# A two-layer hybrid encoder trunk: calls recorded, list-scheduled in the kernel and emitted as one fixed list

## The chip, the core and the metric

One core of one Trainium2 chip runs the whole kernel in one launch. Times are device microseconds of that core. A core has five engines with a queue each: PE (TensorE, matmuls), DVE (VectorE), ACT (ScalarE), POOL (GpSimd) and SP (SyncE, which here only issues DMAs). Each engine takes its instructions in order; between engines they are ordered by semaphores that one instruction raises when it has ended and another waits for.

## The reference, cut to what matters

Two layers (DEPTH = 2) over 512 tokens of width 1024, float32. Each layer is:

```python
h = rms_norm(x, norm_mix[l])
proj = h @ w_in[l]                          # 1024 -> 3224 columns
y_att = attention_mixer(...)                # windowed softmax attention, 6 heads
y_dn  = deltanet_mixer(...)                 # gated DeltaNet, chunked, two directions
y_rw  = rwkv_mixer(...)                     # RWKV-7 time mixing, two directions
x = x + concatenate([y_att, y_dn, y_rw]) @ w_out[l]     # 1024 -> 1024
h = rms_norm(x, norm_ffn[l])
u = depthwise_conv(h @ ffn_w_up[l], conv_w)             # 1024 -> 5632
gate, val = split(u)
x = x + (silu(gate) * val) @ ffn_w_down[l]              # 2816 -> 1024
```

A last `rms_norm` closes the trunk.

## The kernel before, in words

Activations lie transposed: 128 channels on the partitions, 512 tokens along the free axis. Every large product is made column block by column block: for 128 output channels, `weights` loads 512 rows of the weight at a time (256 KB, tile `wr`) by a DMA on SP's queue, ACT rounds it to a high part `wh` (L321), POOL makes the low part `wl` (L322), and `product` issues three matmuls of 128x128 by 128x512 for each 128 rows: `wh` with the high part of the activation (`hh`), `wh` with its low part (`hl`), `wl` with `hh` (L332 to L334). `wr`, `wh` and `wl` have three buffers each. Per layer there are 26 column blocks of the input projection with 8 such triples each, 8 of the output projection with 8, 44 of the up-projection with 8 and 8 of the down-projection with 22: 800 triples, and 4,800 matmuls in both layers.

The stages of a layer follow each other: the input projection for RWKV (`proj`, `token_shift`), `rwkv_prep` twice, `dn_gates`, `dn_proj`, a 32x32 triangular inverse on DVE (`invert`, `finish_inverse`), the eight serial steps of `rwkv_scan`, `dn_prep`, the inverse for DeltaNet (`invert_both`), the eight steps of `dn_scan` with the attention heads beside it, `dn_out`, the output projection, the gated MLP (L1074 to L1097) and the down-projection (L1101 to L1105). The mixers consist of some 3,500 small float32 matmul calls in both layers and of elementwise work on DVE, ACT and POOL.

The order of the work: the code calls the engines directly (`V`, `S`, `G`, `PE`, `nc.sync`), and the framework's `TileContext(nc, auto_bufs=True)` (L1148) orders the calls itself when it closes, engine by engine, by its own cost model; it puts in a wait wherever an instruction reads or overwrites what another one made. Work of different engines and DMAs runs side by side as far as these waits let it.

Of the kernel before, what the change touches and what calls it, by code (L numbers as in the profile page):

```python
# [14 lines left out]
P = 128  # L15
# [99 lines left out]

def trunk(tc, t, out):
    nc = tc.nc
    V, S, G, PE = nc.vector, nc.scalar, nc.gpsimd, nc.tensor
# [16 lines left out]
    def ps(stream, shape=(P, T)):  # L135
        return psp.tile(list(shape), F32, tag="ps" + stream, bufs=PS_BUFS[stream], name=nm("ps"))

    def p4(*free, dt=F32):
        return bp.tile([P, *free], dt, tag="p4", bufs=20, name=nm("p4"))

    def t2(stream, *free, dt=F32):
        return bp.tile([P, *(free or (T,))], dt, tag="t" + stream, bufs=T_BUFS[stream], name=nm("t" + stream))

    def cv(*free, dt=F32):
        return bp.tile([P, *(free or (T,))], dt, tag="cv", bufs=8, name=nm("cv"))

    def at_(*free, dt=F32):
        return bp.tile([P, *(free or (T,))], dt, tag="at", bufs=5, name=nm("at"))
# [3 lines left out]
    def sm(*free):  # L152
        n = math.prod(free)
        a = bp.tile([P, T], F32, tag="sm", bufs=7, name=nm("sm"))[:, :n]
        return a.rearrange("p (a b) -> p a b", b=free[1])
# [3 lines left out]
    def tiny(*free, tag="tiny"):  # L159
        if len(free) > 1:  # L160
            lo = W + DEPTH * NPAR + 2 * T + 48 * small_at.setdefault(tag, len(small_at))
            names = " ".join("abc"[: len(free)])
            return fixed[:, lo : lo + math.prod(free)].rearrange(f"p ({names}) -> p {names}", **dict(zip("abc", free)))
        return bp.tile([P, *free], F32, tag=tag, bufs=1 if len(free) > 1 else 3, name=nm(tag))
# [7 lines left out]
    nc.sync.dma_start(par[:, :, :n1], t["params"][:, :, :n1])  # L172
# [30 lines left out]

    def late_params():
        nc.sync.dma_start(cst[:, n0:], t["consts"][:, n0:])
        nc.sync.dma_start(par_all[:, :, n1:], t["params"][:, :, n1:])
        for l in range(DEPTH):
            nc.sync.dma_start(sinkb[l], t["attn_sink"][l].unsqueeze(0).broadcast_to([P, 6]))
# [19 lines left out]
    def exp_ln_tables():  # L228
        tc.keep_in_program_order(S.preload_act_table_set("natural_log_exp_and_others"))
# [7 lines left out]

    def rotary_tables():
        pi_ = t2("d", T, dt=I32)
        nc.sync.dma_start(pi_, t["positions"].broadcast_to([P, T]))  # L240
# [21 lines left out]
    def split(src, gcol, tag, k):  # L262
        hi = bp.tile([P, T], F32R, tag=f"hh{k}", bufs=1, name=nm("hh"))
        lo = bp.tile([P, T], F32R, tag=f"hl{k}", bufs=1, name=nm("hl"))
        if gcol is None:
            S.activation(hi, src, AF.Copy)
            V.tensor_tensor(lo, src, hi.bitcast(F32), sub)
        else:
            S.activation(hi, src, AF.Copy, scale=gcol)
            V.scalar_tensor_tensor(lo, src, gcol, hi.bitcast(F32), mult, sub)  # L270
        return hi, lo

    class Norm:
# [32 lines left out]
    def weights(pieces, nk, m=P):  # L306


        parts = []
        for k0 in range(0, nk, WK):  # L310
            k1 = min(nk, k0 + WK)
            n = k1 - k0
            if ahead:
                raw = ahead.pop(0)
            else:
                raw = bp.tile([P, WK, m], F32, tag="wr", bufs=3, name=nm("wr"))
                for dst, src in pieces(raw[:, :n, :], k0, k1):
                    nc.sync.dma_start(dst, src)
            hi = bp.tile([P, WK, m], F32R, tag="wh", bufs=3, name=nm("wh"))
            lo = bp.tile([P, WK, m], F32R, tag="wl", bufs=3, name=nm("wl"))  # L320
            S.activation(hi[:, :n, :], raw[:, :n, :], AF.Copy)  # L321
            G.tensor_tensor(lo[:, :n, :], raw[:, :n, :], hi[:, :n, :].bitcast(F32), sub)  # L322
            parts += [(hi[:, k, :], lo[:, k, :]) for k in range(n)]
        return parts

    def product(o, w, x):


        n = len(w)
        for k in range(n):  # L330
            (wh, wl), (xh, xl) = w[k], x[k]
            PE.matmul(o, wh, xh, start=k == 0, stop=False)  # L332
            PE.matmul(o, wh, xl, start=False, stop=False)  # L333
            PE.matmul(o, wl, xh, start=False, stop=k == n - 1)  # L334

    def proj(l, parts, c0, m=P, heads=None):
# [53 lines left out]

    def invert(dpk, upper, E, work):
# [29 lines left out]

    def invert_both(dpks, work):
# [21 lines left out]

    def finish_inverse(st, o1, o2, units, upper, sign):
# [25 lines left out]

    def token_shift(l, o, i, rb, dst):
# [6 lines left out]

    def rwkv_prep(l, pr_, st, wau):  # L480
# [35 lines left out]
        nc.sync.dma_start(st["aside"][:, pr_, :], bv)  # L516
# [84 lines left out]

    def rwkv_scan(st):
# [56 lines left out]

    def rwkv_out(l, st, pr_, dst):  # L660
        y = st["y"][:, pr_, :]
        bv, g = t2("r"), t2("r")
        nc.sync.dma_start(bv, st["aside"][:, pr_, :])
        nc.sync.dma_start(g, st["aside"][:, 2 + pr_, :])
# [32 lines left out]

    def dn_gates(l, o, rb, scr, st):
# [19 lines left out]
        nc.scalar.dma_start(scr[0:6], rt[0:6])  # L718
        nc.scalar.dma_start(scr[6:12], rt[38:44])
# [9 lines left out]

    def dn_prep(l, pr_, st, qkv, nb, scr):  # L730
# [13 lines left out]
        for hh in range(2):  # L744
            nc.scalar.dma_start(e[64 * hh : 64 * hh + 64], sv[2 * pr_ + hh].unsqueeze(0).broadcast_to([64, 2, T]))
# [31 lines left out]

    def dn_scan(st):
# [71 lines left out]

    def dn_out(l, st, pr_, zs):
# [21 lines left out]

    def attn_head(l, tq, q, k, vt, dst):
# [37 lines left out]
    def layer(l, norm, xd, last):  # L912
# [9 lines left out]
        for i in range(8):  # L922
# [6 lines left out]
            if i == 3:  # L929
                wau = bp.tile([P, 2, 256], F32, tag="wau", name=nm("wau"))  # L930
                nc.sync.dma_start(wau[0:64], t["rw_w_up"][l].rearrange("d r c -> r d c"))
                nc.sync.dma_start(wau[64:128], t["rw_a_up"][l].rearrange("d r c -> r d c"))
                gup = bp.tile([P, T], F32, tag="gup", name=nm("gup"))[:, :256]
                nc.sync.dma_start(gup, t["rw_g_up"][l])
# [7 lines left out]
        for pr_ in range(2):  # L942
# [4 lines left out]
            nc.sync.dma_start(rw["aside"][:, 2 + pr_, :], g)  # L947
# [3 lines left out]

        def attn_proj():
# [18 lines left out]

        def gate_proj(pr_, z):
# [11 lines left out]

        def dn_proj(pr_):
# [69 lines left out]
        for j in range(KT):  # L1055
# [9 lines left out]
            nc.sync.dma_start(xo, xd[:, j, :])  # L1065
# [47 lines left out]
    for l in range(DEPTH):  # L1113
        x, norm = layer(l, norm, xd, l == DEPTH - 1)
        xd = xdram
        if l < DEPTH - 1:
            for k in range(KT):
                nc.sync.dma_start(xd[:, k, :], x[k])
    nfw = at["norm_final"]
    for k in range(KT):  # L1120
        V.scalar_tensor_tensor(x[k], x[k], par[0][:, nfw + k : nfw + k + 1], norm.rb, mult, mult)
        nc.sync.dma_start(out[:, k, :], x[k])
# [29 lines left out]
```

## Time and profile before

| | |
|---|---|
| median of three runs | 1716.09 us (1713.92 to 1722.8) |
| the profiled execution | 1722.8 us, span 1721.0 us |
| granted TensorE clock, mean over the span | 0.931 of full speed |
| PE busy | 1544.2 us |
| DVE / ACT / POOL busy | 973.5 / 792.0 / 638.7 us |
| mixers of layer 0, then of layer 1 | 0 to 464 us, 866 to 1306 us |
| up-projection with the gated MLP, layer 0 | 508 to 746 us |

The span is from the first to the last instruction; what lies around it is 1.8 us. Busy times of the engines overlap each other, so their sum is far above the span. A matmul's record overlaps the next one's, since matmuls are pipelined: the distance between starts tells the rate. In views by stretch, PEclk is the mean granted clock as a share of full speed; 1.00 is 2.4 GHz and 0.50 is 1.2 GHz. A line such as L322 is the line of the kernel that issued the instruction.

### The profile page before, as it was taken

What the parts mean: (1) busy time and instruction counts of PE and PEld (TensorE: products, weight loads), DVE (VectorE), ACT (ScalarE), POOL (GpSimd) and SP (SyncE); (2) the same over time, 40 slices, a digit from 0 to 9 for tenths busy, and PEclk for the clock granted to TensorE, in tenths of its full rate; (3) what the DMA queues carried; (4) which work ended last, traced back from release to release, by engine and by line L of the source; (5) the groups of instructions that cost most, each with busy time, mean ns of one, the idle gap of its engine ahead of it and who ended that gap; (6) DMA issues with size and microseconds to landing.
All of it is one profiled execution on the core that took longest, in us unless ns stands there. A gap on an engine that the chain in (4) does not pass through costs nothing. (4 is left out here: it accounts for less than half of the span.)

```text
span 1721.0 us, 29049 instructions
## 1 busy us (share of the span) xinstructions
PE 1544.2 (90%) x11500; PEld 1208.7 (70%) x11500; DVE 973.5 (57%) x1595; ACT 792.0 (46%) x1493; POOL 638.7 (37%) x510
## 2 busy tenths in 40 slices
PE   7988889569999999999998887983899999999997
PEld 4676666347778888888876666652677788888885
DVE  6578946875535557731136797579563555555001
ACT  5547453355444444433336654351734544444321
POOL 4321323101265554445552112420104555555553
PEclk9989979669999999999999998995799999999998
DMA  6221211100143333333442012220003333333331
GB/s 185 73 57 38 56 38 44 37 2 20 36 122 96 98 98 95 96 104 114 119 101 68 25 45 50 55 70 1 4 19 93 102 95 97 98 99 114 101 101 65
DMA packets 230536, 126.07 MB, mean 73 GB/s; under 512 B 23656, under 2 KB 221416, under 8 KB 230400
## 3 DMA queue, kind: packets, MB, share of 16 engines
q1 hardware_dynamic: 228624, 121.02, 25.0%
q10 hardware_dynamic: 1776, 3.20, 0.6%
q8 instruction: 90, 1.47, 0.3%
q14 instruction: 46, 0.38, 0.1%
HBM read 117.84 MB, written 6.34 MB: 72 GB/s over the span
## 5 line engine op out<-in xcount | busy, mean ns | idle before, releaser
L322 POOL TENSOR_TENSOR wl<-wr,wh 128x512 fp32r<-128x512 f32 (+1 forms) x408 | 553.6, 1363 | 753.2 <-ACT wh L321 664.2
L332 PE MATMUL ps<-hh,wh 128*128 128x512 f32 x1248 | 505.2, 405 | 22.1 <-ACT wh L321 19.6
L333 PE MATMUL ps<-hl,wh 128*128 128x512 f32 x1248 | 504.5, 404 | 0.0
L334 PE MATMUL ps<-hh,wl 128*128 128x512 f32 x1248 | 500.9, 401 | 0.4 <-POOL wl L322 0.4
L321 ACT ACTIVATE wh<-wr 128x512 fp32r<-128x512 f32 (+1 forms) x408 | 246.2, 615 | 330.8 <-PE ps L333 262.4
L332 PEld LDWEIGHTS ps<-hh,wh 128*128 128x128 f32 x1248 | 237.8, 191 | 80.9 <-ACT wh L321 20.4
L333 PEld LDWEIGHTS ps<-hl,wh 128*128 128x128 f32 x1248 | 238.0, 191 | 56.8 <-issue 4.2
L334 PEld LDWEIGHTS ps<-hh,wl 128*128 128x128 f32 x1248 | 237.5, 190 | 56.8 <-issue 3.9
L1104 DVE TENSOR_TENSOR p<-ps,p 128x512 f32<-128x512 f32 x16 | 11.1, 692 | 196.6 <-PE ps L334 196.6
L332 PE MATMUL ps<-p,wh 128*128 128x512 f32 x256 | 99.6, 389 | 0.0
L333 PE MATMUL ps<-p,wh 128*128 128x512 f32 x256 | 99.6, 389 | 0.0
L334 PE MATMUL ps<-p,wl 128*128 128x512 f32 x256 | 99.6, 389 | 0.0
L903 PE MATMUL ps<-fixed,cv 128*128 128x128 f32 x120 | 24.9, 340 | 62.4 <-DVE cv L900 62.0
L1081 DVE TENSOR_TENSOR tr<-ps,rb 128x512 f32<-128x512 f32 x44 | 30.4, 691 | 80.9 <-PE ps L334 80.8
L292 POOL TENSOR_TENSOR tr<-tr,tr 128x512 f32<-128x512 f32 x32 | 42.6, 1332 | 70.4 <-ACT tr L285 59.9
L903 PEld LDWEIGHTS ps<-fixed,cv 128*128 128x128 f32 x120 | 16.0, 168 | 72.5 <-issue 44.8
L1084 DVE SCALAR_TENSOR_TENSOR td<-tr,fixed,td 128x511 f32<-128x511 f32 x44 | 42.8, 972 | 37.7 <-ACT td L1083 37.7
L285 ACT ACTIVATE tr<-p 128x512 f32<-128x512 f32 x36 | 22.6, 628 | 85.9 <-DVE p L1104 64.4
L791 POOL TENSOR_TENSOR sm<-sm,fixed 128x384 f32<-128x384 f32 x12 | 10.8, 896 | 121.5 <-DVE sm L820 64.5
L333 PEld LDWEIGHTS ps<-p,wh 128*128 128x128 f32 x256 | 48.1, 188 | 10.1
L332 PEld LDWEIGHTS ps<-p,wh 128*128 128x128 f32 x256 | 48.1, 188 | 10.1
L1084 DVE SCALAR_TENSOR_TENSOR tr<-td,fixed,tr 128x511 f32<-128x511 f32 x44 | 33.9, 771 | 37.5 <-ACT tr L1083 37.5
(294 smaller groups left out, 2559.7 us busy)
## 6 DMA issues: line engine op xcount, KB each, us to landing
wr<-ffn_w_up SPq DMA_DIRECT2D x176, 256.0 KB, 2.8
wr<-w_in SPq DMA_DIRECT2D x88, 256.0 KB, 2.9
wr<-ffn_w_down SPq DMA_DIRECT2D x80, 256.0 KB, 2.9
wr<-w_in SPq DMA_DIRECT2D x24, 128.0 KB, 2.4
p<-scr ACTq DMA_DIRECT2D x12, 256.0 KB, 3.5
wr<-w_out SPq DMA_DIRECT2D x32, 96.0 KB, 2.6
wr<-w_out SPq DMA_DIRECT2D x16, 192.0 KB, 2.9
p<-xt SPq DMA_DIRECT2D x8, 256.0 KB, 5.0
```

Of the source, the lines that this page charges most:

```text
L285: S.activation(sq, xk, AF.Square)
L292: G.tensor_tensor(acc, self.acc, sq, add)
L321: S.activation(hi[:, :n, :], raw[:, :n, :], AF.Copy)
L322: G.tensor_tensor(lo[:, :n, :], raw[:, :n, :], hi[:, :n, :].bitcast(F32), sub)
L332: PE.matmul(o, wh, xh, start=k == 0, stop=False)
L333: PE.matmul(o, wh, xl, start=False, stop=False)
L334: PE.matmul(o, wl, xh, start=False, stop=k == n - 1)
L791: G.tensor_tensor(gs, state, flat(gl, step), mult)
L903: PE.transpose(pp[:, P * j : P * j + P], scs[g][:, P * j : P * j + P], ident)
L1081: V.tensor_tensor(u, o, nf.rb, mult)
L1084: V.scalar_tensor_tensor(a[:, 1:], u[:, :-1], w(0), a[:, 1:], mult, add)
L1104: V.tensor_tensor(x1[j], o, x1[j], add)
```

## The change

The engines' handles become recorders: a call is not issued but kept in a list with the tiles that it reads and writes (`Plan.add`). At the end `Plan.schedule` works out the dependencies and a price for each call, places the calls by a list scheduler with a lead per task (`LEAD`, a table of 38 numbers) and a budget of memory, and gives back one list, sorted by the planned start. `Plan.emit` then makes the calls in that order. The tiles for the high and low parts of the activations get two buffers instead of one, `weights` becomes a generator, and pools share their memory through the planner. The arithmetic and the number of instructions that do it stay: 8,278 matmul calls, 553 DMAs and the same calls on DVE, ACT and POOL.

The program is now built with `linearize=True`. In the built program each instruction then waits for the end of the instruction that stands before it in the one list, whichever engine that one is on; for a DMA that is the landing of its data. Only between two matmuls that follow each other on PE no wait is written. Of 6,563 neighbours in the list that are on different engines, 6,556 carry this wait; in the program before it is 12. The list changes from PE to another engine 2,812 times, so its matmuls stand in 2,812 runs; 1,925 of the runs end with a matmul of `product`, 886 with a small one.

```diff
+LEAD = {
+    "attn_head1": 81000, "attn_head2": 65800, "attn_proj": 240100, "dn_gates": 19600, "dn_out0": 129900, "dn_out1": 256800,
...
+class Plan:
...
+        self.room = {"ps": 8, "sb": 148000, "wr": 3, "wh": 3, "wl": 3}
...
+    def tile(self, pool, shape, dtype, tag, bufs, name):
+        a = pool.tile(list(shape), dtype, tag=tag, bufs=bufs if tag in self.room else 64, name=name)
...
+    def add(self, eng, call, args, kw):
+        o = _Op()
+        o.n, o.eng, o.call, o.args, o.kw = len(self.ops), eng, call, args, kw
...
+        for o in ops:
+            o.left, o.ready, o.prio = len(o.deps), 0.0, -o.rank - self.lead.get(o.group, 0)
...
+        return sorted(order, key=lambda o: (o.start, o.n))
+
+    def emit(self):
+        for o in self.schedule():
+            o.call(*o.args, **o.kw)
+
+
+class _Recorder:
+    def __init__(self, plan, eng, obj):
+        self._plan, self._eng, self._obj = plan, eng, obj
+
+    def __getattr__(self, name):
+        f, plan, eng = getattr(self._obj, name), self._plan, self._eng
+        return lambda *a, **k: plan.add(eng, f, a, k)
...
-    V, S, G, PE = nc.vector, nc.scalar, nc.gpsimd, nc.tensor
+    plan = Plan(tc.nc)
+    V, S, G, PE, SY = (_Recorder(plan, e, o) for e, o in (("DVE", tc.nc.vector), ("ACT", tc.nc.scalar), ("POOL", tc.nc.gpsimd), ("PE", tc.nc.tensor), ("SP", tc.nc.sync)))
...
-        hi = bp.tile([P, T], F32R, tag=f"hh{k}", bufs=1, name=nm("hh"))
+        hi = plan.tile(bp, [P, T], F32R, tag=f"hh{k}", bufs=2, name=nm("hh"))
...
+    plan.emit()
     ctx.close()
...
-    with _tile.TileContext(nc, auto_bufs=True) as tc:
+    with _tile.TileContext(nc, auto_bufs=True, linearize=True) as tc:
```

Three places, with the semaphores that each row waits for in brackets (a semaphore named after an engine is raised by each instruction of that engine, one named DMAHW by the DMAs that use it). First SP's queue at the start of the program, before: the tiles `p` are the eight pieces of the input, `fixed` holds parameters and constants.

```order
L193 DMA p_68<-xt 128x512
L172 DMA fixed<-params 128x2x61
L193 DMA p_68<-xt 128x512
L193 DMA p_69<-xt 128x512 x2
L198 DMA wr_77<-w_in 128x4x128
L193 DMA p_70<-xt 128x512
```

and now:

```order
L486 DMA p_67<-xt 128x512 [waits Pool_49]
L486 DMA p_68<-xt 128x512 [waits DMAHW1_49]
L486 DMA p_68<-xt 128x512 [waits DMAHW2_49]
L486 DMA fixed<-params 128x2x61 [waits DMAHW3_49]
L486 DMA p_69<-xt 128x512 [waits DMAHW4_49]
L486 DMA p_69<-xt 128x512 [waits DMAHW5_49]
```

Before, these DMAs were issued one behind the other; now each waits until the one before it has landed. Second DVE at the start, where it works out small constants from the parameters, before:

```order
L216 TENSOR_TENSOR fixed<-fixed 128x8 [waits DMAHW1_49]
L218 TENSOR_SCALAR fixed<-fixed 128x2
L219 TENSOR_SCALAR fixed<-fixed 128x2
L217 TENSOR_SCALAR fixed<-fixed 128x8 [waits DVE_49]
L220 TENSOR_SCALAR fixed<-fixed 128x4
```

and now:

```order
L486 TENSOR_TENSOR fixed<-fixed 128x8 [waits Activation_49]
L486 TENSOR_SCALAR fixed<-fixed 128x8 [waits Activation_49]
L486 TENSOR_SCALAR fixed<-fixed 128x4 [waits Pool_49]
L486 TENSOR_SCALAR fixed<-fixed 128x4 [waits DVE_49]
L486 TENSOR_SCALAR fixed<-fixed 128x2 [waits DVE_49]
```

None of these uses anything that ACT or POOL made; the waits name the engine of the instruction that stands before each in the list. All rows now have the line of `emit`, L486. Third PE in the up-projection of layer 0, before: one column block, `ps` its accumulator.

```order
L332 MATMUL ps_6253<-hh_4479,wh_6256 128x512 [waits DVE_49,Activation_49]
L333 MATMUL ps_6253<-hl_4480,wh_6256 128x512
L334 MATMUL ps_6253<-hh_4479,wl_6257 128x512 [waits Pool_49]
L332 MATMUL ps_6253<-hh_4528,wh_6256 128x512
L333 MATMUL ps_6253<-hl_4529,wh_6256 128x512
L334 MATMUL ps_6253<-hh_4528,wl_6257 128x512
```

and now:

```order
L486 MATMUL ps_1106<-hh_905,wl_1112 128x512 [waits DMAHW5_49]
L486 MATMUL ps_1106<-hh_917,wh_1111 128x512 [waits Activation_49]
L486 MATMUL ps_1116<-hh_858,wh_1118 128x512 [waits Pool_49]
L486 MATMUL ps_1116<-hl_859,wh_1118 128x512
L486 MATMUL ps_1106<-hl_918,wh_1111 128x512 [waits Activation_49]
L486 MATMUL ps_1106<-hh_917,wl_1112 128x512
L486 MATMUL ps_1106<-hh_929,wh_1111 128x512
L486 MATMUL ps_1106<-hl_930,wh_1111 128x512 [waits DVE_49]
L486 MATMUL ps_1116<-hh_858,wl_1119 128x512 [waits DMAHW6_49]
```

Before, a block's first matmuls waited for its weights and the rest followed without a wait; now the matmuls of two blocks alternate in short runs, and each run waits for an instruction of another engine or for the landing of a DMA (of a weight that a later block uses).

## Rows read from the trace of the kernel before

**Rows 1.** The page's first part: busy us, share of the span, instructions.

```profile
span 1721.0 us, 29049 instructions
...
PE 1544.2 (90%) x11500; PEld 1208.7 (70%) x11500; DVE 973.5 (57%) x1595; ACT 792.0 (46%) x1493; POOL 638.7 (37%) x510
```

**Rows 2.** By stretch: length, then busy us (instructions) by engine, granted clock, DMA share, GB/s.

```profile
516.00:559.00 43.00, 43.00 (x191) 35.61 (x190) 24.10 (x33) 20.55 (x32) 22.67 (x16) 1.00 0.33 98
508.00:746.00 238.00, 238.00 (x1047) 197.00 (x1046) 149.34 (x172) 111.47 (x175) 120.29 (x87) 1.00 0.33 96
322.00:371.00 49.00, 22.09 (x140) 13.85 (x140) 45.30 (x112) 13.60 (x42) 0.21 (x1) 0.57 0.00 1
216.00:238.00 22.00, 15.46 (x283) 11.71 (x283) 5.10 (x6) 12.83 (x30) 1.27 (x1) 0.51 0.04 13
389.00:452.00 63.00, 59.95 (x1043) 46.99 (x1039) 38.17 (x121) 31.16 (x86) 8.37 (x8) 0.96 0.05 15
70.00:166.00 96.00, 82.49 (x750) 62.86 (x749) 72.95 (x97) 61.56 (x115) 20.27 (x14) 0.89 0.21 55
...
0.00:464.00 464.00, 381.00 (x4015) 280.48 (x4016) 325.98 (x606) 232.75 (x488) 111.63 (x98) 0.88 0.20 53
866.00:1306.00 440.00, 364.99 (x3996) 271.79 (x3997) 302.18 (x571) 219.77 (x465) 96.73 (x88) 0.88 0.16 43
```

**Rows 3.** DMA issues: transfer, queue, count, KB each, median us from issue to landing.

```profile
wr<-ffn_w_up SPq DMA_DIRECT2D x176, 256.0 KB, 2.8
wr<-w_in SPq DMA_DIRECT2D x88, 256.0 KB, 2.9
wr<-ffn_w_down SPq DMA_DIRECT2D x80, 256.0 KB, 2.9
...
tr<-aside SPq DMA_DIRECT2D x8, 256.0 KB, 3.8
wr<-w_out SPq DMA_DIRECT2D x32, 64.0 KB, 2.2
```

**Rows 4.** The same for the weight loads of line L318 alone.

```profile
DMA to landing us min/median/max: 1.9/2.8/7.3
```

**Rows 5.** Timeline, 0 to 32 us: start us, duration us, engine, line, operation.

```profile
8.57 0.63 ACT L321 ACTIVATE wh<-wr 128x512 fp32r<-128x512 f32 x1
...
9.24 0.29 PEld L332 LDWEIGHTS ps<-hh,wh 128*128 128x128 f32 x1 [9.24 <-ACT wh L321]
...
21.92 0.63 PE L332 MATMUL ps<-hh,wh 128*128 128x512 f32 x1
...
22.35 0.63 PE L333 MATMUL ps<-hl,wh 128*128 128x512 f32 x1
```

**Rows 6.** Timeline, 142 to 145.6 us.

```profile
142.67 0.80 PE L332 MATMUL ps<-hh,wh 128*128 128x512 f32 x1 [4.73 <-ACT wh L321]
```

**Rows 7.** Timeline, 461.5 to 464.5 us.

```profile
463.28 0.51 PE L333 MATMUL ps<-hl,wh 128*128 128x512 f32 x1
```

**Rows 8.** Timeline, 540 to 545.5 us.

```profile
539.76 0.63 ACT L321 ACTIVATE wh<-wr 128x512 fp32r<-128x512 f32 x1 [1.09 <-PE ps L333]
...
540.47 1.78 POOL L322 TENSOR_TENSOR wl<-wr,wh 128x512 fp32r<-128x512 f32 x1 [1.43 <-ACT wh L321]
...
543.19 1.30 POOL L322 TENSOR_TENSOR wl<-wr,wh 128x512 fp32r<-128x512 f32 x1 [0.94 <-ACT wh L321]
543.50 0.72 ACT L1083 ACTIVATE tr<-td,fixed 128x512 f32<-128x512 f32 x1 [0.39 <-DVE td L1081]
...
544.26 0.78 DVE L1084 SCALAR_TENSOR_TENSOR tr<-td,fixed,tr 128x511 f32<-128x511 f32 x1 [0.85 <-ACT tr L1083]
```

**Rows 9.** Groups of instructions: count, then busy us, mean ns, idle before.

```profile
L322 POOL TENSOR_TENSOR wl<-wr,wh 128x512 fp32r<-128x512 f32 (+1 forms) x408 | 553.6, 1363 | 753.2 <-ACT wh L321 664.2 <-issue 47.4 <-PE ps L334 20.8
...
L1084 DVE SCALAR_TENSOR_TENSOR td<-tr,fixed,td 128x511 f32<-128x511 f32 x44 | 42.8, 972 | 37.7 <-ACT td L1083 37.7
...
L1084 DVE SCALAR_TENSOR_TENSOR tr<-td,fixed,tr 128x511 f32<-128x511 f32 x44 | 33.9, 771 | 37.5 <-ACT tr L1083 37.5
```

More of the change, by code (lines that the diff above doesn't have):

```diff
@@ L135, in ps @@
     def ps(stream, shape=(P, T)):
-        return psp.tile(list(shape), F32, tag="ps" + stream, bufs=PS_BUFS[stream], name=nm("ps"))
+        return plan.tile(psp, list(shape), F32, tag="ps" + stream, bufs=PS_BUFS[stream], name=nm("ps"))
     def p4(*free, dt=F32):
-        return bp.tile([P, *free], dt, tag="p4", bufs=20, name=nm("p4"))
+        return plan.tile(bp, [P, *free], dt, tag="p4", bufs=20, name=nm("p4"))
     def t2(stream, *free, dt=F32):
-        return bp.tile([P, *(free or (T,))], dt, tag="t" + stream, bufs=T_BUFS[stream], name=nm("t" + stream))
+        return plan.tile(bp, [P, *(free or (T,))], dt, tag="t" + stream, bufs=T_BUFS[stream], name=nm("t" + stream))
     def cv(*free, dt=F32):
-        return bp.tile([P, *(free or (T,))], dt, tag="cv", bufs=8, name=nm("cv"))
+        return plan.tile(bp, [P, *(free or (T,))], dt, tag="cv", bufs=8, name=nm("cv"))
     def at_(*free, dt=F32):
-        return bp.tile([P, *(free or (T,))], dt, tag="at", bufs=5, name=nm("at"))
+        return plan.tile(bp, [P, *(free or (T,))], dt, tag="at", bufs=5, name=nm("at"))
     x4 = p4
@@ L163, in tiny @@
             return fixed[:, lo : lo + math.prod(free)].rearrange(f"p ({names}) -> p {names}", **dict(zip("abc", free)))
-        return bp.tile([P, *free], F32, tag=tag, bufs=1 if len(free) > 1 else 3, name=nm(tag))
+        return plan.tile(bp, [P, *free], F32, tag=tag, bufs=1 if len(free) > 1 else 3, name=nm(tag))
     W = _CONST.shape[1]
@@ L202, in trunk @@
     sinkb = [fixed[:, W + DEPTH * NPAR + 2 * T + 288 + 6 * l :][:, :6] for l in range(DEPTH)]
+    @plan.task
     def late_params():
-        nc.sync.dma_start(cst[:, n0:], t["consts"][:, n0:])
-        nc.sync.dma_start(par_all[:, :, n1:], t["params"][:, :, n1:])
+        SY.dma_start(cst[:, n0:], t["consts"][:, n0:])
+        SY.dma_start(par_all[:, :, n1:], t["params"][:, :, n1:])
         for l in range(DEPTH):
-            nc.sync.dma_start(sinkb[l], t["attn_sink"][l].unsqueeze(0).broadcast_to([P, 6]))
+            SY.dma_start(sinkb[l], t["attn_sink"][l].unsqueeze(0).broadcast_to([P, 6]))
     def derive_params():
@@ L306, in weights @@
     def weights(pieces, nk, m=P):
-        parts = []
         for k0 in range(0, nk, WK):
@@ L315, in weights @@
             else:
-                raw = bp.tile([P, WK, m], F32, tag="wr", bufs=3, name=nm("wr"))
+                raw = plan.tile(bp, [P, WK, m], F32, tag="wr", bufs=3, name=nm("wr"))
                 for dst, src in pieces(raw[:, :n, :], k0, k1):
-                    nc.sync.dma_start(dst, src)
-            hi = bp.tile([P, WK, m], F32R, tag="wh", bufs=3, name=nm("wh"))
-            lo = bp.tile([P, WK, m], F32R, tag="wl", bufs=3, name=nm("wl"))
+                    SY.dma_start(dst, src)
+            hi = plan.tile(bp, [P, WK, m], F32R, tag="wh", bufs=3, name=nm("wh"))
+            lo = plan.tile(bp, [P, WK, m], F32R, tag="wl", bufs=3, name=nm("wl"))
             S.activation(hi[:, :n, :], raw[:, :n, :], AF.Copy)
             G.tensor_tensor(lo[:, :n, :], raw[:, :n, :], hi[:, :n, :].bitcast(F32), sub)
-            parts += [(hi[:, k, :], lo[:, k, :]) for k in range(n)]
-        return parts
+            yield from ((hi[:, k, :], lo[:, k, :]) for k in range(n))
     def product(o, w, x):
-        n = len(w)
-        for k in range(n):
-            (wh, wl), (xh, xl) = w[k], x[k]
+        n = len(x)
+        for k, (wh, wl) in enumerate(w):
+            xh, xl = x[k]
             PE.matmul(o, wh, xh, start=k == 0, stop=False)
@@ L334, in product @@
             PE.matmul(o, wl, xh, start=False, stop=k == n - 1)
+    @plan.task
     def proj(l, parts, c0, m=P, heads=None):
@@ L388, in run @@
                 return e.value
+    @plan.task
     def invert(dpk, upper, E, work):
@@ L420, in neg_diag32 @@
             V.scalar_tensor_tensor(dst, lo, m[:, 0:1], hi, mult, sub)
+    @plan.task
     def invert_both(dpks, work):
@@ L443, in invert_both @@
         return res
+    @plan.task
     def finish_inverse(st, o1, o2, units, upper, sign):
@@ L478, in token_shift @@
         V.scalar_tensor_tensor(dst[:, :-1], u[:, 1:], par[l][:, mu + 8 + i : mu + 9 + i], dst[:, :-1], mult, add)
+    @plan.task
     def rwkv_prep(l, pr_, st, wau):
@@ L600, in both @@
         return a[:, :, c : NCH - c : NCH - 1 - 2 * c, :], step >= NCH // 2
+    @plan.task
     def rwkv_scan(st):
@@ L658, in rwkv_scan @@
             yield
+    @plan.task
     def rwkv_out(l, st, pr_, dst):
@@ L662, in rwkv_out @@
         bv, g = t2("r"), t2("r")
-        nc.sync.dma_start(bv, st["aside"][:, pr_, :])
-        nc.sync.dma_start(g, st["aside"][:, 2 + pr_, :])
+        SY.dma_start(bv, st["aside"][:, pr_, :])
+        SY.dma_start(g, st["aside"][:, 2 + pr_, :])
         pm = ps("r")
@@ L696, in dn_conv @@
         V.tensor_tensor(dst, dst, sg, mult)
+    @plan.task
     def dn_gates(l, o, rb, scr, st):
@@ L717, in dn_gates @@
         chunk_sums(rt[32:44], rt[64:76], True)
-        nc.scalar.dma_start(scr[0:6], rt[0:6])
-        nc.scalar.dma_start(scr[6:12], rt[38:44])
+        S.dma_start(scr[0:6], rt[0:6])
+        S.dma_start(scr[6:12], rt[38:44])
         pn = ps("d", (P, NCH, 12))
@@ L728, in dn_gates @@
         return nb
+    @plan.task
     def dn_prep(l, pr_, st, qkv, nb, scr):
@@ L776, in dn_prep @@
         st["kv"].append(kv)
+    @plan.task
     def dn_scan(st):
@@ L849, in dn_scan @@
             yield
+    @plan.task
     def dn_out(l, st, pr_, zs):
@@ L872, in rope @@
         V.tensor_tensor(dst, dst, q, add)
+    @plan.task
     def attn_head(l, tq, q, k, vt, dst):
@@ L929, in layer @@
             if i == 3:
[L930 to L934, printed above, removed]
+                wau = plan.tile(bp, [P, 2, 256], F32, tag="wau", bufs=1, name=nm("wau"))
+                SY.dma_start(wau[0:64], t["rw_w_up"][l].rearrange("d r c -> r d c"))
+                SY.dma_start(wau[64:128], t["rw_a_up"][l].rearrange("d r c -> r d c"))
+                gup = plan.tile(bp, [P, T], F32, tag="gup", bufs=1, name=nm("gup"))[:, :256]
+                SY.dma_start(gup, t["rw_g_up"][l])
         if l == 0:
@@ L946, in layer @@
             S.activation(g, pg, AF.Copy)
-            nc.sync.dma_start(rw["aside"][:, 2 + pr_, :], g)
+            SY.dma_start(rw["aside"][:, 2 + pr_, :], g)
         rw["pc"] = tiny(2, 2, NCH, tag="pc")
         rw["dpk"] = p4(32, 32)
+        @plan.task
         def attn_proj():
@@ L970, in attn_proj @@
                 yield q
+        @plan.task
         def gate_proj(pr_, z):
@@ L983, in layer @@
         scr = dp.tile([12, T], F32, name=nm("scr"))
+        @plan.task
         def dn_proj(pr_):
@@ L1064, in layer @@
             xo = t2("r")
-            nc.sync.dma_start(xo, xd[:, j, :])
+            SY.dma_start(xo, xd[:, j, :])
             o = ps("j")
@@ L1117, in trunk @@
             for k in range(KT):
-                nc.sync.dma_start(xd[:, k, :], x[k])
+                SY.dma_start(xd[:, k, :], x[k])
     nfw = at["norm_final"]
```

348 lines of the change are left out of this document (334 added, 14 removed), and 5 rows, old and new, of the table LEAD.

## The prediction

> **What bounds the kernel now.** I read the page's busy times first, then the views by stretch, the DMA issues, the timeline at single instructions, and the groups by line; the question for each was how much of the work lies beside other work, because the change decides about that and about nothing else.
>
> The busy times [rows 1] add up to far more than the span: PE 1544.2, DVE 973.5, ACT 792.0 and POOL 638.7 make 3,948 us of work in 1721.0 us, before a single DMA is counted. PE alone is busy for 90% of the span. The stretch views [rows 2] show where: in the up-projection PE is busy for all of 43.00 us with 191 matmuls, one per 0.225 us, at granted clock 1.00 (2.4 GHz), while DVE, ACT and POOL each work for half of the time and the weight loads take a DMA share of 0.33, all of it beside the matmuls. The same holds for the whole 238 us of that stage. So the product stages are bound by PE, and everything else there is hidden. In the mixers the limit changes from stage to stage: 322 to 371 us is bound by DVE (45.30 of 49), 389 to 452 us by PE (59.95 of 63), 216 to 238 us by nothing for long (PE 15.46 and ACT 12.83 of 22), which is a chain that passes from engine to engine. There is thus little idle time for a better order to take, and very much overlap for a worse one to lose.
>
> **What the change does to the order.** The planner's list alone would be another arrangement of the same parallel work. But each instruction is now emitted with a wait for the end of the one before it in the list, on whatever engine. The three places of the order show it. On SP the pieces of the input, which were issued one behind the other, now each wait for the DMA queue's semaphore that the previous piece raises when it has landed. On DVE the constants, four of which had no wait on another engine, now wait for ACT, POOL or the previous DVE instruction. On PE the product matmuls stand in runs of one to a few, and each run waits, among others for the landing of a weight that only a later block needs. What is queued behind a waiting instruction on its engine cannot pass it, and what stands behind it on other engines waits for it in turn: there is one chain, and its length is the sum of all parts. No lead and no second buffer can give overlap back, since only neighbours on PE have no wait between them.
>
> **The sum.** It is made against the profiled execution, 1722.8 us (span 1721.0 and 1.8 around it), which is the slowest of the three runs; the median is 1716.09. Against a sum of this size the 7 us are nothing.
>
> *DMAs.* Each of the 553 is now awaited to its landing by the next instruction. The weight loads take 2.8 us (176 of the up-projection) and 2.9 us (88 + 80) [rows 3]: 176 x 2.8 + 168 x 2.9 = 980. Of the other 209 the rows show 2.2 to 3.8, I take 2.7: 564. Together 1,544 us. The lower bound is the fastest weight load seen, 1.9 [rows 4], for all: 1,051; an upper one is 3.2 for each, half a microsecond above what I took, 1,770. A load that is alone has no neighbour to share with, which speaks for the lower side; one that is started from an idle queue has its issue in the chain, which speaks for the upper. I stay with the medians.
>
> The Trainium skill, page "DMA: Bandwidth & Descriptors", section "Anatomy of one DMA — SWDGE (gpsimd) path", puts a transfer at a fixed part of about 2.0 us and its bytes over 436 GB/s; for 256 KB that is 2.6 us, an estimate from that page, against the 2.8 of the row, and the sum would be some 70 us lower by it (344 loads by 0.2). Its section "Rules for kernel authors" says to issue a DMA early and to wait late so that the fixed part is covered; the change does the opposite for every transfer, and [rows 3] is what each then lays bare.
>
> *DVE, ACT and POOL.* Their 973.5 + 792.0 + 638.7 = 2,404 us [rows 1] no longer lie beside anything. Some instructions got longer because of a neighbour: POOL's L322 takes 1363 ns in the mean [rows 9] and 1.30 us in the shorter of two cases [rows 8]; the two forms of L1084 on DVE, of one shape, take 972 and 771 ns [rows 9]. Alone they should be at the short end, 2,330 in all. Against that a record's end may not be when its successor starts: 2,500. I take 2,404.
>
> *PE.* 4,800 product matmuls and the small ones. What a matmul costs depends on the clock: 0.225 us in a row at 1.00 [rows 2], but 0.43 where the clock is at its lower level, from start to start (21.92, 22.35) [rows 5]. Which of the two will be granted? In the stretch where PE worked 22.09 of 49 us the clock was 0.57, where it worked 15.46 of 22 it was 0.51, where it worked 59.95 of 63 it was 0.96 [rows 2]. In the chain PE works less than half of the time, in short pieces, so I take the first two rows: 1.2 GHz nearly throughout. Then 4,800 x 0.43 = 2,064. The last matmul of a run is now seen to its end: alone one takes 0.80 [rows 6], so 0.37 on top for each of 1,925 runs, 712. The small matmuls are what is left of PE's busy time, 1544.2 - 4,800 x 0.225 = 464; they stand in the mixers, whose granted clock is 0.88 [rows 2], so 408 at full clock and 816 at half. PE in all: 2,064 + 712 + 816 = 3,592. At full clock throughout it would be 1,080 + 1,925 x (0.51 - 0.225) [rows 7] + 408 = 2,037, so the clock is worth some 1,555 us.
>
> *Handoffs.* A wait across engines has its own price. From ACT to DVE: 543.50 + 0.72 to 544.26, 0.04; from ACT to POOL: 539.76 + 0.63 to 540.47, 0.08 [rows 8]; from ACT to PE's weight load: 8.57 + 0.63 to 9.24, 0.04 [rows 5]. With 0.05, between these, for 6,563 changes: 328. Some 350 waits of DVE, ACT and SP on themselves at about 0.035: 12. Together 340, bounds 200 and 600 (0.03 and 0.09 each).
>
> In all 1,544 + 2,404 + 3,592 + 340 = 7,880, and with the 1.8 around the span 7,882. Some of PE's work, in the longer runs of the mixers, will find the full clock; I give a tenth of the 1,555 back, 156, and forecast **7,730 us**. With every term at its low end and the full clock the sum is 1,051 + 2,330 + 2,037 + 200 = 5,618; with all at the high end 1,770 + 2,500 + 3,592 + 600 = 8,462.
>
> The parts of the change with no price of their own: the second buffers of the activations' parts, the shared memory and the leads change only which instruction stands where in the list. What they would hide is hidden behind nothing, since nothing runs beside anything.
>
> **The rivals.**
>
> *The clock stays high.* The same chain, but PE gets 2.4 GHz for most of it: 7,882 - 1,555 = 6,327 if always, 7,200 if for somewhat under half. For it: [rows 2] show 1.00 wherever products follow each other, and the list has some long runs of small matmuls. Against it: the rows with PE at 45% and 70% of the stretch. A chance of 0.2.
>
> *The chain is dearer.* Handoffs of 0.1 to 0.15 instead of 0.05 add 330 to 650, or a DMA from an idle queue costs 0.5 more, 277: 8,400 to 9,000. For it: the 3.8 and 2.9 us of some transfers [rows 3]. Against it: the short handoffs of [rows 8]. 0.07.
>
> *The waits cost nothing, the order decides.* It ends on the other side. If the added waits were nearly always met already, so that engines still ran side by side, only the planner's order would count. The place is the chain-like stretches: 216 to 238 us (and its like in layer 1) could fall towards its busiest engine, PE at half clock or ACT at 12.83, up to 9 us each, 18; 70 to 166 us has DVE at 72.95 of 96 [rows 2], so up to 23 each, of which a half, 23 in all; 389 to 452 us has 3 us of idle PE and some products that could go elsewhere, 6 each, 12. 1,722.8 - 53 = 1,670, and a little less if the clock gains too, about 1,655 (1,610 to 1,721). It decides as soon as a wait on a list neighbour is met before the engine comes to it. Against it: the neighbour is by construction the instruction that itself waited for its own neighbour, so the wait cannot have been met earlier. 0.03, which covers that I misread what the built program does.
>
> **How the numbers follow.** The chain at half clock, 7,300 to 8,400, has 0.70; the full clock for much of it 0.20; the dear chain 0.07; the free waits 0.03. The range of 6,600 to 8,400 holds the first, the upper half of the second, and so about 0.8. Faster by more than 0.5% (about what a measurement of this kernel can tell from no change) is the last rival alone, 0.02; within 0.5% 0.01; slower 0.97.
>
> **What would show it right or wrong.** PE, DVE, ACT, POOL and the exposed DMA time should add up to the span, with PE at some 45% of it and the others at 8 to 13% each; granted clock near 0.5 in nearly every slice; product matmuls 0.43 apart in a run and 0.80 alone; the DMA share below 0.10; idle time before every group ended by whichever instruction stands before it in the list, often one that has nothing to do with its data; weight loads at 2.7 us, none of them beside a matmul; the chain spread over all engines and the DMAs. All lines read L486. If PE's share is that but the clock reads 0.8 or more, the first rival holds. If the busy times overlap as in [rows 1], the reading of the waits is wrong, and with it the whole sum.

## The result: 4.53 times slower, and the profile after

The changed kernel takes 7786.06 us (median of four runs, 7773.58 to 7790.5), the kernel before 1716.9 (now a median of four): a ratio of 4.532, interval 4.519 to 4.545. The forecast was 7,730, the range 6,600 to 8,400. The profiled execution took 7785.79 us, its span 7783.9. The page's first part of the kernel after, in the columns of [rows 1]:

```profile
span 7783.9 us, 29901 instructions
...
PE 3591.4 (46%) x11500; PEld 1862.8 (24%) x11500; DVE 916.0 (12%) x1595; ACT 839.6 (11%) x1493; POOL 584.2 (8%) x510
```

Each of these engines executes as many instructions as in [rows 1], but PE's share has fallen from 90% to 46% while its time has more than doubled. From the page's second part, the granted clock and the DMAs' share in 40 slices, in tenths:

```profile
PEclk9555555555555555555555555555555555555555
DMA  1000000000000000000000000000000000000000
```

After the first slice every slice stands close to the lower level, 0.50 (the first is dealt with under *The clock* below); the DMA engines are nearly idle throughout. The DMA issues of the kernel after, in the columns of [rows 3]:

```profile
wr<-ffn_w_up SPq DMA_DIRECT2D x176, 256.0 KB, 2.8
wr<-w_in SPq DMA_DIRECT2D x88, 256.0 KB, 2.7
wr<-ffn_w_down SPq DMA_DIRECT2D x80, 256.0 KB, 2.8
p<-scr ACTq DMA_DIRECT2D x12, 256.0 KB, 3.5
wr<-w_in SPq DMA_DIRECT2D x24, 128.0 KB, 2.2
```

With no other transfer beside them the large weight loads land hardly sooner than before (2.8, 2.9 and 2.9 in [rows 3]). The medians of all rows of this view, each by its count, add up to some 1,450 us. What one sees in the up-projection is the timeline of the kernel after (start, duration, engine; in brackets the idle time and what ended it; weight loads inside a run and some rows before the last four left out):

```profile
3000.92 0.79 PE L486 MATMUL ps<-hh,wl 128*128 128x512 f32 x1 [2.86 <-DMA wr<-ffn_w_up]
...
3001.51 0.63 PE L486 MATMUL ps<-hh,wh 128*128 128x512 f32 x1
...
3001.94 0.63 PE L486 MATMUL ps<-hl,wh 128*128 128x512 f32 x1
3002.60 0.75 DVE L486 SCALAR_TENSOR_TENSOR tr<-td,fixed,tr 128x511 f32<-128x511 f32 x1 [6.25 <-PE ps L486]
3003.41 0.29 PEld L486 LDWEIGHTS ps<-hh,wl 128*128 128x128 f32 x1 [1.56 <-DVE tr L486]
3003.41 0.80 PE L486 MATMUL ps<-hh,wl 128*128 128x512 f32 x1 [0.84 <-DVE tr L486]
...
3004.00 0.63 PE L486 MATMUL ps<-hh,wh 128*128 128x512 f32 x1
3004.72 0.63 ACT L486 ACTIVATE wh<-wr 128x512 fp32r<-128x512 f32 x1 [16.73 <-PE ps L486]
...
3005.40 0.80 PE L486 MATMUL ps<-hl,wh 128*128 128x512 f32 x1 [0.77 <-ACT wh L486]
3006.23 0.75 DVE L486 SCALAR_TENSOR_TENSOR td<-tr,fixed,td 128x511 f32<-128x511 f32 x1 [2.88 <-PE ps L486]
...
3014.32 0.63 PE L486 MATMUL ps<-hl,wh 128*128 128x512 f32 x1
3015.02 0.37 SPq L486 DMA_DIRECT2D wr<-ffn_w_up  x1
3017.90 0.29 PEld L486 LDWEIGHTS ps<-hh,wl 128*128 128x128 f32 x1 [3.67 <-DMA wr<-ffn_w_up]
```

Each row of another engine begins, within 0.1 us, where the one above it ends. The DVE instruction at 3002.60 prepares another tile than the matmul after it reads, and that matmul waits for it all the same. Between two engines stand 0.03 (3001.94 + 0.63 to 3002.60), 0.06 (3002.60 + 0.75 to 3003.41) or 0.09 us (3004.00 + 0.63 to 3004.72). Inside a run the second matmul starts 0.59 behind the first, the next ones 0.43 apart, and the last takes 0.63: three take 1.65 (3000.92 to 3001.94 + 0.63). One that is alone takes 0.80, as in [rows 6]. The forecast's 0.43 for each and 0.37 for the end of a run give 1.66 and 0.80. From the load's issue at 3015.02 until PE goes on at 3017.90, no engine works. The view of waits sums this up (engine, what was waited for: us in total, times, longest):

```profile
POOL wl L486 <- PE ps L486: 3230.5, 234, 113.7
...
DVE p L486 <- POOL wl L486: 621.0, 18, 118.9
...
PEld ps L486 <- DMA wr<-ffn_w_up: 654.0, 165, 5.8
```

`wl` is made from weights, so POOL needs nothing that a matmul gives, except that the buffer's last reader has ended; in [rows 9] its idle time ended with ACT's `wh`. And DVE's `p` does not read `wl` at all.

### The profile page after: what moved, and what is told of

It reads as the page before. It is cut to its first block, busy times and chain, and to the rows that moved or that the text cites. A ratio compares the mean times of both kernels' runs of the same rounds, so it can differ in the third digit from the quotient of the medians.

```text
span 7783.9 us, 29901 instructions
## 1 busy us (share of the span) xinstructions
PE 3591.4 (46%) x11500; PEld 1862.8 (24%) x11500; DVE 916.0 (12%) x1595; ACT 839.6 (11%) x1493; POOL 584.2 (8%) x510
## 5 line engine op out<-in xcount | busy, mean ns | idle before, releaser
L486 PE MATMUL ps<-hh,wl 128*128 128x512 f32 x1248 | 859.9, 703 | 1202.8 <-DMA wr<-ffn_w_up 531.0
L486 PE MATMUL ps<-hh,wh 128*128 128x512 f32 x1248 | 849.6, 693 | 719.4 <-POOL wl L486 254.8
L486 PE MATMUL ps<-hl,wh 128*128 128x512 f32 x1248 | 817.9, 681 | 542.2 <-DVE tr L486 109.7
L486 POOL TENSOR_TENSOR wl<-wr,wh 128x512 fp32r<-128x512 f32 (+1 forms) x408 | 502.2, 1231 | 5871.3 <-PE ps L486 3230.5
L486 PEld LDWEIGHTS ps<-hh,wl 128*128 128x128 f32 x1248 | 376.2, 303 | 1650.2 <-DMA wr<-ffn_w_up 619.0
L486 PEld LDWEIGHTS ps<-hh,wh 128*128 128x128 f32 x1248 | 378.4, 305 | 1084.3 <-POOL wl L486 348.2
L486 ACT ACTIVATE wh<-wr 128x512 fp32r<-128x512 f32 (+1 forms) x408 | 251.8, 617 | 3243.5 <-PE ps L486 2856.5
L486 PEld LDWEIGHTS ps<-hl,wh 128*128 128x128 f32 x1248 | 380.9, 311 | 869.4 <-DVE tr L486 173.3
L486 PE MATMUL ps<-p,wh 128*128 128x512 f32 x512 | 311.5, 665 | 269.5 <-DMA wr<-ffn_w_down 98.0
L486 PE MATMUL ps<-p,wl 128*128 128x512 f32 x256 | 168.0, 656 | 201.2 <-DMA wr<-ffn_w_down 173.2
L486 PEld LDWEIGHTS ps<-p,wh 128*128 128x128 f32 x512 | 152.9, 307 | 399.8 <-DMA wr<-ffn_w_down 115.8
L486 PE MATMUL ps<-p,p 32*32 32x32 f32 (+2 forms) x1232 | 129.4, 326 | 208.3 <-DVE p L486 69.5
L486 PE MATMUL ps<-sm,p 64*64 64x64 f32 x1344 | 119.9, 321 | 126.5 <-DMA wr<-w_out 23.3
L486 PE MATMUL ps<-p,sm 64*64 64x64 f32 x1200 | 119.0, 319 | 114.1 <-DVE sm L486 20.9
L486 DVE TENSOR_TENSOR p<-ps,p 128x512 f32<-128x512 f32 (+2 forms) x72 | 40.2, 558 | 973.6 <-POOL wl L486 571.6
L486 PEld LDWEIGHTS ps<-p,p 32*32 32x32 f32 (+1 forms) x1232 | 85.9, 178 | 254.7 <-DVE p L486 79.8
L486 PEld LDWEIGHTS ps<-p,wl 128*128 128x128 f32 x256 | 79.4, 310 | 256.6 <-DMA wr<-ffn_w_down 165.0
L486 DVE TENSOR_TENSOR td<-ps,rb 128x512 f32<-128x512 f32 (+1 forms) x64 | 44.2, 691 | 766.1 <-PE ps L486 746.7
L486 PEld LDWEIGHTS ps<-sm,p 64*64 64x64 f32 x1344 | 92.8, 215 | 166.9 <-issue 31.2
L486 PE MATMUL ps<-fixed,cv 128*128 128x128 f32 x168 | 60.7, 450 | 148.6 <-DVE cv L486 66.6
L486 PEld LDWEIGHTS ps<-p,sm 64*64 64x64 f32 x1200 | 90.0, 212 | 143.8 <-DVE sm L486 28.7
L486 DVE SCALAR_TENSOR_TENSOR td<-tr,fixed,td 128x511 f32<-128x511 f32 x88 | 66.1, 751 | 446.6 <-PE ps L486 380.3
```

The lines of the kernel that those rows point to most:

```text
L486: o.call(*o.args, **o.kw)
```

## The experiments

Two theories stood against each other: the waits between list neighbours make one chain, and its parts add up (mine); or the planner's order, its leads and its memory budget cost the time. The second to the sixth run below (from the chain on the kernel before to the filled chain) were executed once each; four executions of the changed kernel lie within 0.2% of each other, those of the kernel before within 1%.

**The order alone.** The option is left out, and each call is pinned behind the previous call on its own engine. On each of the five engines the order is that of the changed kernel, instruction for instruction.

```diff
         for o in self.schedule():
-            o.call(*o.args, **o.kw)
+            i = o.call(*o.args, **o.kw)
+            if i is not None:
+                self.tc.keep_in_program_order(i)
...
-    with _tile.TileContext(nc, auto_bufs=True, linearize=True) as tc:
+    with _tile.TileContext(nc, auto_bufs=True) as tc:
```

> The planner's list is kept on every engine, instruction for instruction, but each instruction waits only for what it reads or overwrites. Theory (the added waits make one chain; the order by itself is harmless): 1,610 to 1,721 us, about 1,655, PE busy for 90% of the span again, granted clock above 0.9. Rival (the planner's order or its memory budget is what costs): well above 1,800, with engines waiting for buffers, and only part of the 6,070 us comes back.

Measured: 1710.52 us, ratio to before 0.9961, interval 0.9938 to 0.9983. Its busy times:

```profile
span 1707.2 us, 28989 instructions
...
PE 1550.9 (91%) x11500; PEld 1200.5 (70%) x11500; DVE 1017.1 (60%) x1595; ACT 789.9 (46%) x1493; POOL 631.5 (37%) x510
```

PE is at 91% and the overlap is back. So all of the 6,070 us are the waits; the planned order itself, with its buffers, saves 5.6 us or 0.4%. That is at the weak end of the 1,610 to 1,721 that were expected, 55 us above the likely value of 1,655, and still this version is the fastest that was measured here.

**The chain on the kernel before.** Only the option is set in the kernel before.

```diff
-    with _tile.TileContext(nc, auto_bufs=True) as tc:
+    with _tile.TileContext(nc, auto_bufs=True, linearize=True) as tc:
```

> The kernel before, in its own program order, with each instruction waiting for the one before it in the program. It has 607 runs of matmuls instead of 2,812 and 3,288 changes of engine instead of 6,563. Theory: the same DMA time (1,455), the same DVE, ACT and POOL time (2,340), PE 2,064 + 816 + 607 x 0.37 = 3,105 at half clock, 165 of handoffs: 7,065 us, some 720 below the changed kernel, or 5,510 if the longer runs get the full clock. Rival (the planner's list is at fault, not the chain): far below 5,500, towards the 1,717 of before.

Measured: 6229.09 us, between the two values expected; the rival's 1,717 is out. Its busy times, and a piece of its timeline in the up-projection, where 24 product matmuls follow each other:

```profile
PE 2190.4 (35%) x11500; PEld 1602.5 (26%) x11500; DVE 916.5 (15%) x1595; ACT 839.6 (13%) x1493; POOL 584.4 (9%) x510
```

```profile
2001.25 0.63 PE L332 MATMUL ps<-hh,wh 128*128 128x512 f32 x1
2001.68 0.63 PE L333 MATMUL ps<-hl,wh 128*128 128x512 f32 x1
2002.11 0.52 PE L334 MATMUL ps<-hh,wl 128*128 128x512 f32 x1
2002.47 0.40 PE L332 MATMUL ps<-hh,wh 128*128 128x512 f32 x1
2002.71 0.39 PE L333 MATMUL ps<-hl,wh 128*128 128x512 f32 x1
2002.93 0.39 PE L334 MATMUL ps<-hh,wl 128*128 128x512 f32 x1
...
2018.94 0.80 PE L332 MATMUL ps<-hh,wh 128*128 128x512 f32 x1 [13.55 <-POOL wl L322]
2019.53 0.63 PE L333 MATMUL ps<-hl,wh 128*128 128x512 f32 x1
```

The starts go from 0.43 apart to 0.23 apart within the run, and after 13.55 us without a matmul the next run begins at the low level again. That is why the sum came out between half and full clock (mean 0.619). DVE, ACT and POOL take the same time as in the changed kernel to within 0.5 us. So under a chain the planner's list is the worse one: 7,786 - 6,229 = 1,557 us, of which PE 3,591 - 2,190 = 1,401. The planner's list has 2,812 runs of matmuls instead of 607, so more ends of runs to wait for and fewer matmuls at the higher clock. In the traces 1,925 runs end with a product instead of 172, which at the forecast's 0.37 for an end is some 650 of the 1,401 us, an estimate; the rest was not taken apart, and the lower clock, 0.525 instead of 0.619, is its likely cause.

**Each weight load twice.**

```diff
             o.call(*o.args, **o.kw)
+            if o.call.__name__ == "dma_start" and any(t.startswith("wr") for t in o.tiles):
+                o.call(*o.args, **o.kw)
```

> The changed kernel with each of its 468 weight loads issued twice into the same tile, one behind the other. Theory (each load is awaited to its landing and nothing hides it): the medians of the changed kernel's loads add up to 1,231 us for the 468, so about 7,786 + 1,231 = 9,017 us. Rival (the loads are largely hidden, the handoffs and the clock are the cost): under 8,200, 0.4 to 0.9 per extra load for its issue alone.

Measured: 9034.65 us, 1,249 more for 468 loads, 2.67 each, where the medians gave 2.63. PE's busy time stays:

```profile
PE 3590.5 (40%) x11500; PEld 1864.1 (21%) x11500; DVE 916.5 (10%) x1595; ACT 839.6 (9%) x1493; POOL 584.4 (6%) x510
```

Nothing hides a load, and the load's time is a term of the sum.

**The chain without its loads.** To the pinned order of the first run the waits between neighbours are added by hand, so that the DMAs can be left out of them (`sync` is a dependency with a wait).

```diff
...
+            self.tc.keep_in_program_order(i)
+            if last is not None and not (o.eng == "PE" and last[0] == "PE"):
+                self.tc.add_manual_dep(i.ins, last[1], sync, reason="chain")
+            if o.call.__name__ != "dma_start":
+                last = (o.eng, i.ins.name)
...
```

> The list in the same order and the same chain of waits between the instructions of PE, DVE, ACT and POOL, but no instruction waits for a DMA only because it stands behind it; a DMA still waits for what stands before it, and whoever reads its data waits for its landing. Theory: the exposed DMA time (some 1,455 us) and its 553 handoffs (28) go: about 6,300 us, PE busy for 57% of it; lower still if the clock then rises. Rival (DMA time is hidden in the chain anyway): 7,600 or more.

Measured: 6068.62 us, 1,717 less than the changed kernel where 1,483 were expected.

```profile
PE 3369.6 (56%) x11500; PEld 1806.8 (30%) x11500; DVE 916.6 (15%) x1595; ACT 839.7 (14%) x1493; POOL 584.4 (10%) x510
```

Of the 234 that are missing from the expectation, 222 are PE's: its busy time fell from 3,591 to 3,370. The expectation left room for this ("lower still if the clock then rises"), and the mean granted clock did rise, from 0.525 to 0.547: without the 2.8 us pauses some runs get the full clock, and 374 product matmuls instead of 99 start less than 0.3 us behind the one before them. But a load that no longer stands in the chain also no longer divides a run: the trace has 2,705 runs instead of 2,811, which at the forecast's 0.37 for an end is some 39 us of the 222, an estimate.

**The clock.** Two runs. The first is the chain once more, with all waits written out as in the run before, those for DMAs too, and planned for seven PSUM banks; the second adds, behind each instruction that is not PE's, matmuls that nobody needs, into the eighth bank.

```diff
-        self.room = {"ps": 8, "sb": 148000, "wr": 3, "wh": 3, "wl": 3}
+        self.room = {"ps": 7, "sb": 148000, "wr": 3, "wh": 3, "wl": 3}
...
+            loaded += o.call.__name__ == "dma_start" and o.args[1].tensor.name == "consts"
+            if o.eng != "PE" and loaded == 2:
+                for _ in range(int((2600 if o.call.__name__ == "dma_start" else o.cost) / 250)):
+                    self.tc.keep_in_program_order(self.nc.tensor.matmul(self.spare, self.ident, self.ident, start=True, stop=True))
```

> The chain of the changed kernel, made by a wait written between list neighbours instead of the context's option, and planned with seven PSUM banks instead of eight, so that one is free for the run that follows. It is the comparison for that run. Theory (only the chain counts, not how it is asked for nor the exact list): within 1.5% of 7,786, that is 7,670 to 7,900 us, clock 0.52 to 0.53. Rival (the option does something beside these waits): clearly off that.

> The previous run's kernel, and behind each instruction of DVE, ACT, POOL or SP some matmuls that nothing needs (128x128 of a constant with itself, float32, into the spare bank): one for each 0.25 us that the planner gives the instruction, ten behind a DMA, 12,772 in all. They wait for nothing of the chain. Theory (PE's 3,591 us are half-clock because PE stands idle between short runs): PE stays busy, the clock goes to 0.9 or more, the work of the list on PE falls from 3,591 to some 2,040, the rest of the chain (4,190) stays, and each of 2,800 runs waits for the end of a matmul that nobody needs, 0.1 on average: 6,200 to 6,800 us, faster although 12,772 matmuls were added. Rival (the clock is low for another reason, such as the serial waits themselves): the matmuls take twice as long as the time they are meant to fill, the chain waits for them, and it is slower than 7,786, towards 9,000.

Measured: 7740.07 and 6466.57 us. The first, 0.6% below the changed kernel, shows that the chain and not the option is the cause. The second is faster by 1,274 us with 12,772 matmuls more. Its row by stretch (the columns of [rows 2]), and a piece of its timeline; L497 is the added line, and each of its calls counts as two:

```profile
3000.00:4000.00 1000.00, 828.90 (x5607) 690.58 (x5608) 122.04 (x196) 132.44 (x224) 94.21 (x80) 0.98 0.08 22
```

```profile
3003.55 2.39 PE L497 MATMUL spare<-fixed 128*128 128x128 f32 x20
3003.78 0.37 SPq L487 DMA_DIRECT2D wr<-ffn_w_down  x1
3006.52 0.73 PE L487 MATMUL ps<-p,wh 128*128 128x512 f32 x2 [0.58 <-DMA wr<-ffn_w_down]
3007.09 0.39 PE L487 MATMUL ps<-p,wl 128*128 128x512 f32 x1
3007.32 0.62 PE L487 MATMUL ps<-p,wh 128*128 128x512 f32 x2
```

The mean granted clock is 0.966 instead of 0.529, and product matmuls are 0.23 apart even in short runs. The waits of the chain are the same in both runs, so the low clock came from PE standing still between short runs. What it cost, the matmuls of the chain alone tell (L487, over the whole span, without the added ones):

```profile
0.00:6464.80 6464.80, 2215.24 (x11500) 1167.90 (x11500) 917.46 (x1595) 839.90 (x1493) 586.46 (x506) 0.97 0.07 20
```

They are busy for 2,215 us instead of the 3,555 in the run without the added ones: 1,340, where the prediction put 1,555 on the step between the levels. Of the 1,340 the kernel gained 1,274. Most of the difference is waits for the end of a needless matmul: added up from the traces, the pauses from the end of another engine's instruction to PE's next matmul of the chain grew from 134 to 175 us, those in which a DMA is issued from 1,503 to 1,523.

**The order without its leads.** The order alone, with the table empty.

```diff
-... "rwkv_out": 2, "dn_out": 3}, LEAD
+... "rwkv_out": 2, "dn_out": 3}, {}
```

> The run with the order alone (1,710.5 us), with an empty table of leads: tasks are placed by the rank of their dependencies alone. If the leads are what brings the order level with the kernel before: 1,730 to 1,800, with less overlap of the attention and DeltaNet tasks with products. If the leads decide little: 1,700 to 1,725.

Measured: 1883.13 us, ratio 1.0981, interval 1.0927 to 1.1035: more than either case said. In the view of waits, PE's longest sum in the order with leads and then in the one without:

```profile
PE ps L486 <- DVE cv L486: 50.4, 12, 13.0
```

```profile
PE ps L486 <- DVE p L486: 143.2, 15, 37.5
```

With the leads, PE's waits for DVE's `p` are short:

```profile
PE ps L486 <- DVE p L486: 15.9, 18, 5.5
```

Without them there are fifteen waits of 143.2 us in all, up to 37.5 each; that no product could have been placed there was not shown. PE's idle time grew from 156 to 295 us (span less busy time). The leads are worth 173 us of this planner's order, and without them it loses to the order of the kernel before. No run chains the order without its leads; where nothing overlaps, a lead has nothing to place beside anything.

## Why the prediction was right

The mechanism was the one forecast: one chain, whose length is the sum of its parts. That the number came within 0.7% is in part luck: the DMAs and the elementwise work were put 158 us too high, and against that stood 156 us given back for a clock that did not rise and 63 too little for the handoffs. Term by term, by the profile after:

| term | forecast | measured |
|---|---|---|
| DMAs | 1,544 | 1,450, by the medians |
| DVE, ACT, POOL | 2,404 | 916.0 + 839.6 + 584.2 = 2,340 |
| PE at half clock | 3,592 | 3,591 |
| given back for stretches at full clock | -156 | next to nothing |
| handoffs | 340 | 403, what is left of the span |

- *DMAs.* 94 too high by the medians: 68 of it are the other 209, put at 2.7 and landing in 2.4 in the mean (2.2 for 128 KB of `w_in`; the pieces of the input 2.6, where the kernel before had 5.0), 26 the 344 large loads. The doubled loads confirm the price by themselves. The 2.6 us that the prediction sets beside the row from the Trainium skill is, by the title of the section that it names, for DMAs issued by GpSimd; these loads are issued by SP.
- *DVE, ACT and POOL.* 64 too high. The lower bound, 2,330, was the better value, though the rows that it is drawn from give only some 35 us less than 2,404 (408 x 0.063 + 44 x 0.201). L322 takes 1,231 ns in the mean instead of 1,363 [rows 9], and both forms of L1084, here in one group with L1085, now take 751:

```profile
L486 POOL TENSOR_TENSOR wl<-wr,wh 128x512 fp32r<-128x512 f32 (+1 forms) x408 | 502.2, 1231 | 5871.3 <-PE ps L486 3230.5
...
L486 DVE SCALAR_TENSOR_TENSOR td<-tr,fixed,td 128x511 f32<-128x511 f32 x88 | 66.1, 751 | 446.6 <-PE ps L486 380.3
```

  ACT is busy for 48 us more than before, but not with more work: the times of its instructions add up to 841 us in the trace before and 844 in the one after. Before, they overlapped each other, and busy time counts an overlap once.
- *PE.* The total is right, partly by luck. In the trace after, the matmuls that read `wh` or `wl` are busy for 2,709 us and the small ones for 889; the forecast had 2,064 + 712 = 2,776 and 816. So products were 67 too dear and the small matmuls 73 too cheap. At full clock the small ones are the term that was off: the filled run has 1,637 for products, the forecast 1,080 + 549 = 1,629, and 588 for the small ones, the forecast 408. The 886 runs that end with a small matmul have no price for their ends in the forecast; whether that is the difference was not looked into.
- *The clock.* The step that failed is the tenth of the 1,555 us that was given back for longer runs: the clock was 0.525 in the mean, 0.60 in the first 1,000 us, and 0.51 to 0.54 after it; of the 4,800 product matmuls 99 start less than 0.3 us behind the one before them:

```profile
0.00:1000.00 1000.00, 423.95 (x1230) 203.35 (x1230) 138.37 (x234) 124.42 (x208) 58.91 (x54) 0.60 0.07 18
...
2000.00:3000.00 1000.00, 468.75 (x822) 233.54 (x821) 88.06 (x122) 91.37 (x139) 93.29 (x74) 0.51 0.06 19
3000.00:4000.00 1000.00, 480.93 (x890) 251.34 (x891) 58.38 (x81) 81.58 (x128) 102.84 (x85) 0.52 0.07 22
```

  Even the 0.60 is no sign of a fast PE. It comes from the first 187 us, which the profile gives as 1.00, and there too the matmuls of a run start 0.43 apart:

```profile
0.00:187.00 187.00, 52.03 (x81) 22.23 (x82) 18.27 (x38) 20.33 (x29) 15.12 (x17) 1.00 0.13 35
187.00:1000.00 813.00, 371.92 (x1151) 181.12 (x1149) 120.09 (x196) 104.09 (x179) 43.80 (x37) 0.51 0.05 14
```

```profile
104.68 0.63 PE L486 MATMUL ps<-hl,wh 128*128 128x512 f32 x1
105.11 0.63 PE L486 MATMUL ps<-hh,wl 128*128 128x512 f32 x1
105.53 0.63 PE L486 MATMUL ps<-hh,wh 128*128 128x512 f32 x1
```

  The same holds for the row from which the prediction read 0.43 [rows 5]: the profile before gives 1.00 for its stretch, 0 to 32 us. That 0.43 belongs to the lower level was right all the same, as 3001.51 to 3001.94 at 0.52 shows. In these first stretches the distance between starts tells more than the granted clock does.

  The rows with PE at 45% and 70% of a stretch [rows 2] were the right ones to go by, and without the correction the sum is 7,882 against 7,785.8.
- *Handoffs.* 63 too low: 403 over 6,563 is 0.061 instead of 0.05; in the chained kernel before, 6,227.3 less 2,190.4, 2,340.5 and 1,450 leaves 246 for 3,288, 0.075. A part of this remainder is DMA time above the medians. Added up from the trace after, the pauses in which no engine works and a DMA is issued take 1,506 us, not 1,450. The pauses from one engine to another without a DMA are 5,615 and take 335 us, 0.060 each (0.045 on the way to DVE, 0.122 to POOL). In the chained kernel before the first are 1,510 us and the second 145 us in 2,417, 0.060 again: a handoff has the same price there, and the 0.075 is DMA time.

Of the rivals, the one with the clock at full speed is what the filled run shows when PE is kept busy, but the change does nothing of the kind. The dearer chain needed 0.1 or more for a handoff, or a DMA dearer by 0.5; both stayed below. Its prices add up to 8,200 to 8,800 us, not to the 8,400 to 9,000 that it states. The one in which the order decides needs the waits removed; it then has its place, with 6 us of gain where it put 61. Which of its stretches gained, and what the second buffers gave, was not looked into.

## What to carry to other kernels

Before anything is weighed in a schedule, see in the built program what each instruction waits for: a wait on the list's neighbour turns every plan into a sum of durations, and then the sum of busy times, the landing of each transfer and one handoff of 0.05 us per change of engine come within 1.5% of the time of both chained kernels here. A plan is kept by pinning the order on each engine and leaving the waits to the data. When PE's granted clock is low, look at its pauses first: its price here was a sixth of the span.

## What the runs showed of the hardware

Matmuls without any use made a kernel faster by 16%, as that run's expectation had it (6,200 to 6,800 us; 6,467 measured): PE was busy for 82% of the span, and the granted clock was 0.966 in the mean over products and mixers together. In a run of 24 matmuls after a pause the clock rose inside the run; in the changed kernel's runs, most of one to three, it hardly ever did (0.51 to 0.54 from 1,000 us on). A 256 KB weight load with no other transfer beside it takes 2.7 to 2.8 us, hardly less than the median beside other loads, 2.8 to 2.9. A handoff between engines cost 0.060 us in the mean in both chained kernels, and 0.122 on the way to POOL in the changed kernel.
